# Sub-LayerNorm statistics of a differential-attention layer: sums of squares on four column tiles of the array, and one transpose for all rows

## The chip, the cores and the metric

The kernel runs on one core of one Trainium2 chip. Time is device microseconds (us) of one execution, from the first to the last instruction and what lies around it; the figure before is the median of three runs. The engines are named as the profile names them: PE (TensorE's matmuls), PEld (its weight loads), DVE (VectorE), ACT (ScalarE), POOL (GpSimd) and SP, the engine whose queue issues most of the DMAs.

## What is computed

Two transformer layers over 512 latent tokens and 256 context tokens of width 1024, each followed by a squared-ReLU MLP. Layer 0 uses windowed attention, layer 1 differential attention. The change is in layer 1, in the normalisation of each head's output over its 128 channels:

```python
a = diff_weights(qblk, k_all).astype(v.dtype)          # softmax 1 - lam * softmax 2
ox = einsum('bhqk,bkhe->bqhe', a, v_all)               # 8 heads of 128 channels
...
o32 = o.astype(jnp.float32)
o32 = o32 * lax.rsqrt(jnp.mean(jnp.square(o32), axis=-1, keepdims=True) + SUBLN_EPS)
o32 = o32 * subln_g * (1.0 - lam_init)
return o32.astype(o.dtype).reshape(B, n, H * 2 * d) @ wo
```

All products run in float32 split in a high and a low part, so that most matmuls come in threes (lines 318 to 320).

## The kernel before

The order of PE's instructions is written out by a small scheduler of the kernel's own (`Flow`). Jobs are Python generators that yield the conditions on which they go on; the scheduler keeps a clock that advances by an estimated cost of each PE step (`fl.pe`, with `mm(n)` for one matmul of n columns) and models the other engines' work by estimated costs as well (`dv`, `ac`, `gp`). At each point the job of the highest priority whose conditions hold by that clock emits its next matmuls. So a changed estimate can change the order of everything behind it. The other engines' instructions are put in order by the framework's own scheduling.

In layer 1 four kinds of job share PE for each of the 8 heads (0 to 7). `proj1` projects the head's Q, K and V, six blocks of 128 tokens with 24 matmuls each (`qkv_ps`, 384 columns wide for the four latent blocks and 256 for the two context blocks). `post1` evicts a block: V, then rope on DVE and POOL, then high and low parts of K (`sk`) and Q (`sq`), which PE transposes (`kT_ps`, line 1229, and `qT_ps`, line 1244). `scores1` makes the scores (`s_ps`, line 1324), their minimum on DVE and their exponential on ACT. `att1` transposes the weights (`pT_ps`, line 1389) and multiplies them with V (`o_ps`, line 1361). While head n is in `att1`, `proj1` and `post1` work on head n+1.

The normalisation ends `att1`. The head's output lies transposed: channels on the 128 partitions, 512 tokens along the free dimension (`oraw`). POOL squares it (`osq`). PE sums over the partitions with a matmul against a column of ones: `selT[:, hg, 0:NG]` has ones in column `hg` alone, so the sum of the first head of a pair (`hg` 0) lands in row 0 and that of the second in row 1 of `rms_ps`, over two partitions and 512 columns (line 1418). DVE copies (first head) or adds (second head) the two rows to `rms_sb`. After the second head of a pair, four transposes bring each 128 tokens of `rms_sb` to the partitions (`rmsT`, line 1432), DVE adds epsilon in `rr`, POOL takes the power -1/2, PE transposes back (`rmsB`), and a matmul spreads each row over the partitions (`rms_bc`), by which DVE scales `oraw`. So `rms_ps` runs 8 times and `rmsT` in four groups.

A side job, `resid1`, works on the residual during the projection of heads 1 to 4, one step after each latent block's `kT_ps`: POOL multiplies and adds in `rs_x`, SP stores the piece (`x_res`) and fetches the next. After every fourth step two vectors are loaded (`rs_g`, `rs_b`) and scaled on DVE, and those loads are issued when POOL has read the old ones.

Of the kernel before, what the change touches and what calls it, by code (L numbers as in the profile page):

```python
# [13 lines left out]
F32 = mybir.dt.float32  # L14
F32R = mybir.dt.float32r
AF = mybir.ActivationFunctionType
ALU = mybir.AluOpType
AX = mybir.AxisListType

P = 128  # L20
# [20 lines left out]
NG = 2  # L41
# [167 lines left out]
def dve(n):  # L209
    return n / 960 + 0.067  # L210
# [6 lines left out]
def pool2(n):  # L217
    return n * 0.0022 + 0.12


def mm(n):
    return max(n / 2400 + 0.003, 0.108)
# [12 lines left out]
def hybrid_block(ctx: ExitStack, tc: tile.TileContext, t: dict, out: bass.AP):  # L235
    nc = tc.nc
# [8 lines left out]
    fl = Flow()  # L245
# [6 lines left out]
    def psm(name):  # L252
        return ps.tile([P, 512], F32, name=name, tag="m", bufs=4)

    def f(x):
        return x.bitcast(F32)


    def dv(n, deps, fn, lat=LAT, **kw):
        fn(**kw)  # L260
        return fl.op("D", dve(n), deps, lat)
# [5 lines left out]
    def gp(us, deps, fn, lat=LAT, **kw):  # L267
        fn(**kw)  # L268
        return fl.op("G", us, deps, lat)
# [11 lines left out]
    def load_const(name, shape, pool=None):  # L281
        tl = (pool or const).tile(shape, F32, name="c_" + name, tag="c_" + name)
        nc.sync.dma_start(out=tl, in_=t[name])
        return tl
# [40 lines left out]
    ident = f(identr)  # L325
# [156 lines left out]
    def split(n, dep, src, hi, lo, a_deps=(), lat=LAT):  # L482
        a = ac(n, [dep] + list(a_deps), nc.scalar.copy, out=hi, in_=src)
        return a, dv(n, [a], nc.vector.tensor_tensor, lat=lat, out=lo, in0=src, in1=f(hi), op=ALU.subtract)
# [62 lines left out]
    def hx_tiles(pool, nm, tok=TOK):  # L547
        return [pool.tile([P, 2, 2, tok], F32R, name=nm, tag="A", bufs=4) for _ in range(4)]
# [621 lines left out]
    apool = ctx.enter_context(tc.tile_pool(name="apool1", bufs=4, reuse_waits="tile"))  # L1170
    late = ctx.enter_context(tc.tile_pool(name="late", bufs=1))
    oT = hx_tiles(apool, "oT1", SEQ)
    selT = load_const("selT", [P, 4, 4])
    id4 = const.tile([4, 4], F32R, name="id4")
    nc.scalar.copy(out=id4, in_=ident[0:4, 0:4])
    sublg = load_const("sublnT", [P, 1])
# [1 line left out]
    with tc.tile_pool(name="attn1", bufs=1, reuse_waits="tile") as pool:  # L1178
# [15 lines left out]
        st = {"att": -1, "S": -1, "proj": -1}  # L1194
# [158 lines left out]
        def att1(hd_, R):  # L1353
# [3 lines left out]
            def av(kp, qp, pt_, _, xi):  # L1357
                for pl, vl in ((0, 0), (0, 1), (1, 0)):
                    for a in range(2):
                        kb = kp * 2 + a  # L1360
                        nc.tensor.matmul(out=po[:, qp * 256:(qp + 1) * 256], lhsT=vt[:, kb, vl],
                                         rhs=pt_[:, pl, a * 256:a * 256 + 256],
                                         start=(kp == 0 and pl == 0 and vl == 0 and a == 0),
                                         stop=(kp == 2 and pl == 1 and a == 1))
                p = fl.pe(6 * mm(256))
                xS1.give(xi, p)
                return p
# [4 lines left out]
            while i < 6 or pend:  # L1372
# [4 lines left out]
                if room():  # L1377
# [7 lines left out]
                    for a in range(2):  # L1385
                        for qi in range(2):
# [3 lines left out]
                                                in_=es[qp * 2 + qi][0][:, kb * P:(kb + 1) * P], identity=ident)  # L1390
                    p = fl.pe(4 * mm(P))
# [9 lines left out]
                else:  # L1401
                    p = av(*pend.pop(0))
# [6 lines left out]
            osq = pool.tile([P, 512], F32, name="osq", tag="oraw", bufs=3)  # L1409
            g = gp(pool2(512), [a], nc.gpsimd.tensor_tensor, out=osq, in0=oraw, in1=oraw, op=ALU.mult)  # L1410
            hg = hd_ % NG
            if hg == 0:
                st["rms"] = pool.tile([NG, 512], F32, name="rms_sb", tag="rms_sb", bufs=1)
            rms_sb = st["rms"]
            yield [g, sm_.ok]
            rp = psm("rms_ps")
            slot = sm_.take()
            nc.tensor.matmul(out=rp[0:NG, :], lhsT=selT[:, hg, 0:NG], rhs=osq, start=True, stop=True)
            p = fl.pe(4 * mm(512))
            if hg == 0:  # L1420
                d = dv(512, [p], nc.vector.tensor_copy, out=rms_sb, in_=rp[0:NG, :])
            else:
                d = dv(512, [p], nc.vector.tensor_tensor, out=rms_sb, in0=rms_sb, in1=rp[0:NG, :], op=ALU.add)
            sm_.give(slot, d)
            raws.append(oraw)
            if hg < NG - 1:
# [1 line left out]
            yield [d, sm_.ok]  # L1428
            pr = psm("rmsT")
            slot = sm_.take()  # L1430
            for qb in range(4):
                nc.tensor.transpose(out=pr[:, qb * NG:qb * NG + NG], in_=rms_sb[:, qb * P:(qb + 1) * P],
                                    identity=ident[0:NG, 0:NG])
            p = fl.pe(4 * mm(NG))
            rr = small.tile([P, 4 * NG], F32, name="rr", tag="rr", bufs=1)
            ep = small.tile([P, 4 * NG], F32, name="ep", tag="ep", bufs=1)
            s0 = st["s0"][hd_ // NG].rearrange("p q g -> p (q g)")
            dv(8, [], nc.vector.scalar_tensor_tensor, out=ep, in0=s0, scalar=EPS, in1=s0, op0=ALU.mult, op1=ALU.mult)
            d = dv(8, [p], nc.vector.scalar_tensor_tensor, out=rr, in0=pr[:, 0:4 * NG], scalar=1.0 / P, in1=ep,
                   op0=ALU.mult, op1=ALU.add)  # L1440
            sm_.give(slot, d)
            g = gp(0.3 + 0.17 * 4 * NG, [d], nc.gpsimd.tensor_tensor, out=rr, in0=rr, in1=mhalf[:, 0:4 * NG], op=ALU.pow)
            yield [g, sm_.ok]
# [4 lines left out]
            p = fl.pe(4 * mm(P))  # L1448
            rh = pool.tile([NG, 512], F32R, name="rh", tag="rms_sb", bufs=1)
            rl = pool.tile([NG, 512], F32R, name="rl", tag="oraw", bufs=3)  # L1450
            _, d = split(512, p, pb[0:NG, :], rh, rl)
            sm_.give(slot, d)
            for g in range(NG):
# [4 lines left out]
                                 start=True, stop=False)  # L1458
                nc.tensor.matmul(out=bc, lhsT=id4[0:NG, g:g + 1].broadcast_to([NG, P]), rhs=rl,
                                 start=False, stop=True)  # L1460
                p = fl.pe(2 * mm(512))
# [3 lines left out]
                       op1=ALU.mult)  # L1465
# [92 lines left out]
def _rope_tables():  # L1558
    rows = SEQ // GRID_W
    row = np.repeat(np.arange(rows, dtype=np.float32), GRID_W)  # L1560
    col = np.tile(np.arange(GRID_W, dtype=np.float32), rows)
    nf = HD // 4
    inv = (np.float32(ROPE_BASE) ** (-np.arange(nf, dtype=np.float32) / np.float32(nf))).astype(np.float32)
    ang = np.concatenate([row[:, None] * inv, col[:, None] * inv], axis=-1)
    c, s = np.cos(ang).astype(np.float32), np.sin(ang).astype(np.float32)

    def lay(a):
        return np.ascontiguousarray(a.reshape(NXB, P, HD).transpose(1, 0, 2))

    return lay(np.concatenate([c, c], -1)), lay(np.concatenate([-s, s], -1))  # L1570


def _layout(i):
    a = {k: np.asarray(v) for k, v in i.items()}
    C = np.ascontiguousarray
    r = {}
    xx = np.concatenate([a["x"][0], a["ctx"][0]], axis=0)
    r["xtok"] = C(xx.reshape(NTB, P, D))
    r["xT"] = C(xx.T.reshape(KT, P, TOK).transpose(1, 0, 2))
    r["cT"] = C(np.stack([a["c"][0], a["c_ctx"]], -1).reshape(KT, P, 2).transpose(1, 0, 2))  # L1580
    r["w_adaT"] = C(a["w_ada"].reshape(2, D, 6, KT, P).transpose(0, 2, 3, 4, 1))
    r["w_ada"] = C(a["w_ada"].reshape(2, 2, 4, P, 6, 4, 256).transpose(0, 4, 5, 1, 3, 2, 6).reshape(2, 6, 4, 2, P, 1024))
    r["badaT"] = C(a["b_ada"].reshape(2, 6, KT, P).transpose(3, 0, 1, 2))
    ln = np.stack([a["ln1_g"], a["ln1_b"], a["ln2_g"], a["ln2_b"]], 1)
    r["lnrow"] = C(ln)
    r["lnT"] = C(ln.reshape(2, 4, KT, P).transpose(3, 0, 1, 2))
    r["a_wkv"] = C(np.concatenate([a["a_wk"][0], a["a_wv"][0]], -1).reshape(2, 4, P, 256).transpose(0, 2, 1, 3)
                   .reshape(2, P, 1024))

    def half(w):  # L1590
        return C(w.reshape(4, 2, P, 2, 512).transpose(3, 0, 2, 1, 4).reshape(2, 4, P, 1024))

    r["a_wq"] = half(a["a_wq"][0])
    r["a_wo"] = half(a["a_wo"][0])
    r["b_wo"] = half(a["b_wo"][0])
    bw = np.stack([a[n][0].reshape(4, 2, P, B_HEADS, P) for n in ("b_wq", "b_wk", "b_wv")], 4)
    r["b_w"] = C(bw.transpose(3, 0, 2, 1, 4, 5).reshape(B_HEADS, 4, P, 768))
    r["w1"] = C(a["mlp_w1"].reshape(2, KT, P, 32, P).transpose(0, 3, 2, 1, 4).reshape(2, 32, P, 1024))
    r["w2"] = C(a["mlp_w2"].reshape(2, 4, 4, 2, P, 2, 512).transpose(0, 1, 5, 2, 4, 3, 6).reshape(2, 4, 2, 4, P, 1024))
    r["a_sink"] = C(a["a_sink"])  # L1600
    r["lamv"] = C(np.stack([a["b_lq1"][0], a["b_lk1"][0], a["b_lq2"][0], a["b_lk2"][0]], 0).reshape(1, 4 * HD))
    r["sublnT"] = C(a["b_subln_g"].reshape(P, 1))
    r["cosT"], r["sinT"] = _rope_tables()
    r["ident"] = np.eye(P, dtype=np.float32)
    q, k = np.arange(P)[:, None], np.arange(P)[None, :]
    z = np.zeros((P, P), np.float32)
    tl = np.where(q > k, np.float32(1e30), np.float32(0)).astype(np.float32)
    tr = np.where(k > q, np.float32(1e30), np.float32(0)).astype(np.float32)
    r["mask"] = C(np.stack([tl, z, tr, z, z, z], 1))
    selT = np.zeros((P, 4, 4), np.float32)  # L1610
    for g in range(4):
        selT[:, g, g] = 1
    r["selT"] = selT
    return r
# [12 lines left out]
```

## Time and profile before

| | |
|---|---|
| median of 3 runs | 1721.53 us (1721.34 to 1722.16) |
| profiled execution | 1723.21 us, its span 1721.4 us |
| TensorE clock granted, mean | 0.986 |
| attention of layer 1 | about 960 to 1310 us of the span |
| first `rms_ps` of heads 0 to 7 starts at | 996.8, 1040.9, 1090.0, 1131.9, 1177.6, 1216.5, 1258.9, 1296.7 us |
| DVE busy from 960 to 1310 | 237.6 us |

Rows of the timeline give the start, the length, the engine, the line and the operation with its tiles, and in brackets the idle time of the engine before the row and what ended it. A row of the grouped views gives the count, the busy time, the mean length in ns and the idle time before. A row of a table of stretches gives the stretch, its length, the busy time and the number of instructions of PE, PEld, DVE, ACT and POOL, then the granted clock, the DMA share and the GB/s. Matmuls overlap in the pipeline, so one of them takes less of PE than its own length; the distance between two starts is what counts.

### The profile page before, as it was taken

What the parts mean: (1) busy time and instruction counts of PE and PEld (TensorE: products, weight loads), DVE (VectorE), ACT (ScalarE), POOL (GpSimd) and SP (SyncE); (2) the same over time, 40 slices, a digit from 0 to 9 for tenths busy, and PEclk for the clock granted to TensorE, in tenths of its full rate; (3) what the DMA queues carried; (4) which work ended last, traced back from release to release, by engine and by line L of the source; (5) the groups of instructions that cost most, each with busy time, mean ns of one, the idle gap of its engine ahead of it and who ended that gap; (6) DMA issues with size and microseconds to landing.
All of it is one profiled execution on the core that took longest, in us unless ns stands there. A gap on an engine that the chain in (4) does not pass through costs nothing.

```text
span 1721.4 us, 23369 instructions
## 1 busy us (share of the span) xinstructions
PE 1640.2 (95%) x9093; PEld 1360.0 (79%) x9093; DVE 962.3 (56%) x1811; ACT 657.8 (38%) x1281; POOL 344.9 (20%) x314
## 2 busy tenths in 40 slices
PE   6899999999999999999999999999989799999998
PEld 4787567788788888878878988888977788888886
DVE  3665677677755544444446767676765543233336
ACT  3455455462223212302316555455551533223230
POOL 1343444200001101243220122220100000203422
PEclk9999999999999999999999999999999899999999
DMA  9111451243433434324323122211132214232321
GB/s 361 38 50 32 147 178 44 98 158 119 159 134 110 147 122 135 111 98 147 98 64 111 50 68 62 68 47 37 47 110 98 99 62 135 74 117 79 111 86 49
DMA packets 57240, 174.74 MB, mean 102 GB/s; under 512 B 7145, under 2 KB 13097, under 8 KB 57129
## 3 DMA queue, kind: packets, MB, share of 16 engines
q1 hardware_dynamic: 57128, 173.25, 29.9%
q8 instruction: 71, 1.16, 0.3%
q14 instruction: 41, 0.33, 0.1%
HBM read 165.32 MB, written 7.90 MB: 101 GB/s over the span
## 4 chain that ended last, share of the span: by engine, by line
PE 74%; DVE 10%; issue 5%; ACT 4%; POOL 3%; DMA 3%; SPq 0%; POOLq 0%; DVEq 0%; ACTq 0%
PE y_ps L320 10%; PE y_ps L319 10%; PE y_ps L318 10%; PE h_ps L318 8%; PE h_ps L319 8%; PE h_ps L320 8%; PE o_ps L1014 2%; PE qkv_ps L318 2%; PE qkv_ps L319 2%; PE qkv_ps L320 2%; PE s_ps L1324 2%; DVE e L260 2%; PE pT_ps L1028 2%; DVE w_l L260 2%; PE s_ps L981 1%
## 5 line engine op out<-in xcount | busy, mean ns | idle before, releaser
L264 ACT CAST w_h<-w_raw 128x1024 fp32r<-128x1024 f32 (+1 forms) x185 | 186.8, 1014 | 431.1 <-PE y_ps L320 214.3
L260 DVE TENSOR_TENSOR w_l<-w_raw,w_h 128x1024 fp32r<-128x1024 f32 (+1 forms) x185 | 222.8, 1210 | 226.5 <-ACT w_h L264 225.9
L319 PE MATMUL y_ps<-w_l,hid 128*128 128x512 f32 x640 | 252.9, 395 | 1.9 <-DVE w_l L260 1.9
L320 PE MATMUL y_ps<-w_h,hid 128*128 128x512 f32 x640 | 252.9, 395 | 0.6 <-DVE hid L260 0.5
L318 PE MATMUL y_ps<-w_h,hid 128*128 128x512 f32 x640 | 253.1, 395 | 0.0
L268 POOL TENSOR_TENSOR relu<-relu 128x768 f32<-128x768 f32 (+1 forms) x48 | 81.4, 1695 | 613.9 <-ACT relu L264 613.9
L320 PE MATMUL h_ps<-hx0m,w_l 128*128 128x256 f32 (+1 forms) x528 | 176.9, 335 | 0.8 <-DVE w_l L260 0.8
L318 PE MATMUL h_ps<-hx0m,w_h 128*128 128x256 f32 (+1 forms) x528 | 177.1, 335 | 0.0
L319 PE MATMUL h_ps<-hx0m,w_h 128*128 128x256 f32 (+1 forms) x528 | 176.8, 335 | 0.0
L319 PEld LDWEIGHTS y_ps<-w_l,hid 128*128 128x128 f32 x640 | 120.4, 188 | 31.1 <-DVE w_l L260 3.2
L320 PEld LDWEIGHTS y_ps<-w_h,hid 128*128 128x128 f32 x640 | 120.4, 188 | 30.2 <-DVE hid L260 1.9
L318 PEld LDWEIGHTS y_ps<-w_h,hid 128*128 128x128 f32 x640 | 120.4, 188 | 28.6 <-ACT hid L264 0.2
L318 PE MATMUL qkv_ps<-w_h,hx 128*128 128x384 f32 (+1 forms) x384 | 128.1, 334 | 0.0
L319 PE MATMUL qkv_ps<-w_l,hx 128*128 128x384 f32 (+1 forms) x384 | 123.5, 322 | 1.2 <-DVE w_l L260 1.2
L320 PE MATMUL qkv_ps<-w_h,hx 128*128 128x384 f32 (+1 forms) x384 | 123.4, 321 | 0.0
L268 POOL TENSOR_TENSOR e<-e,sm 128x512 f32<-128x512 f32 (+2 forms) x96 | 95.6, 1011 | 127.4 <-DVE sm L260 104.2
L318 PE MATMUL h_ps<-hx1m,w_h 128*128 128x512 f32 (+1 forms) x288 | 108.2, 376 | 3.6 <-ACT relu L264 3.6
L320 PEld LDWEIGHTS h_ps<-hx0m,w_l 128*128 128x128 f32 x528 | 100.0, 189 | 12.5 <-DVE w_l L260 1.6
L319 PEld LDWEIGHTS h_ps<-hx0m,w_h 128*128 128x128 f32 x528 | 99.9, 189 | 11.3
L318 PEld LDWEIGHTS h_ps<-hx0m,w_h 128*128 128x128 f32 x528 | 99.9, 189 | 11.1
L319 PE MATMUL h_ps<-hx1m,w_h 128*128 128x512 f32 (+1 forms) x288 | 107.7, 374 | 0.0
L320 PE MATMUL h_ps<-hx1m,w_l 128*128 128x512 f32 (+1 forms) x288 | 107.6, 374 | 0.0
(225 smaller groups left out, 3131.2 us busy)
## 6 DMA issues: line engine op xcount, KB each, us to landing
w_raw<-in_w SPq DMA_DIRECT2D x128, 512.0 KB, 3.4
w_raw<-in_w_adaT SPq DMA_DIRECT2D x56, 512.0 KB, 3.3
w_raw<-in_w_ada SPq DMA_DIRECT2D x24, 512.0 KB, 4.3
w_raw<-in_b_w SPq DMA_DIRECT2D x32, 384.0 KB, 3.2
raw<-in_w_ada SPq DMA_DIRECT2D x16, 512.0 KB, 9.5
w_raw<-in_a_wq SPq DMA_DIRECT2D x8, 512.0 KB, 6.9
w_raw<-in_a_wo SPq DMA_DIRECT2D x8, 512.0 KB, 3.7
w_raw<-in_b_wo SPq DMA_DIRECT2D x8, 512.0 KB, 4.4
```

The lines of the kernel that those rows point to most:

```text
L260: fn(**kw)
L264: fn(**kw)
L268: fn(**kw)
L318: nc.tensor.matmul(out=o, lhsT=lh, rhs=rh, start=start, stop=False)
L319: nc.tensor.matmul(out=o, lhsT=lh, rhs=rl, start=False, stop=False)
L320: last["pe"] = nc.tensor.matmul(out=o, lhsT=ll, rhs=rh, start=False, stop=stop)
L981: nc.tensor.matmul(out=sp[:, 512:512 + CTX], lhsT=q_, rhs=kT[:, kvh, hl, SEQ:TOK], start=(hl == 0), stop=(hl == 1))
L1014: nc.tensor.matmul(out=po[odd * HD:odd * HD + HD, 0:256], lhsT=vv[:, kb, kvh], rhs=pt_[:, odd * 256:odd * 256 + 256], start=(i == 0), stop ...
L1028: nc.tensor.transpose(out=pp[:, c * P:(c + 1) * P], in_=es[j][:, i * P:(i + 1) * P], identity=ident)
L1324: nc.tensor.matmul(out=sp[:, c0:c1], lhsT=qTt[:, tt, hl, qb * P:(qb + 1) * P], rhs=kS[:, tt, c0:c1], start=(hl == 0), stop=(hl == 1))
```

## The change

The sums of squares are computed by four matmuls of 128 columns, one for each block of 128 tokens, in place of one of 512. Each has a stationary operand of 32 columns and writes to 32 partitions of its own, so that the four use the four column strips of the array. `selT` has 32 columns for it, of which column `hg` holds ones; the rows 2 to 31 of each strip are zeros. `rms_sb` becomes 128 partitions by 128 columns: row 32 q + g is head g of the pair, token block q. One 128x128 transpose replaces the four, and `rr` picks the columns 32 q + g.

```diff
-    selT = load_const("selT", [P, 4, 4])
+    selT = load_const("selT", [P, NG, 32])
...
-                st["rms"] = pool.tile([NG, 512], F32, name="rms_sb", tag="rms_sb", bufs=1)
+                st["rms"] = pool.tile([P, P], F32, name="rms_sb", tag="rms_sb", bufs=1)
...
-            nc.tensor.matmul(out=rp[0:NG, :], lhsT=selT[:, hg, 0:NG], rhs=osq, start=True, stop=True)
-            p = fl.pe(4 * mm(512))
+            for qb in range(4):
+                nc.tensor.matmul(out=rp[32 * qb:32 * qb + 32, 0:P], lhsT=selT[:, hg], rhs=osq[:, qb * P:(qb + 1) * P],
+                                 start=True, stop=True)
+            p = fl.pe(4 * mm(128))
             if hg == 0:
-                d = dv(512, [p], nc.vector.tensor_copy, out=rms_sb, in_=rp[0:NG, :])
+                d = dv(128, [p], nc.vector.tensor_copy, out=rms_sb, in_=rp[:, 0:P])
             else:
-                d = dv(512, [p], nc.vector.tensor_tensor, out=rms_sb, in0=rms_sb, in1=rp[0:NG, :], op=ALU.add)
+                d = dv(128, [p], nc.vector.tensor_tensor, out=rms_sb, in0=rms_sb, in1=rp[:, 0:P], op=ALU.add)
...
-            for qb in range(4):
-                nc.tensor.transpose(out=pr[:, qb * NG:qb * NG + NG], in_=rms_sb[:, qb * P:(qb + 1) * P],
-                                    identity=ident[0:NG, 0:NG])
-            p = fl.pe(4 * mm(NG))
+            nc.tensor.transpose(out=pr[:, 0:P], in_=rms_sb, identity=ident)
+            p = fl.pe(mm(P))
...
-            d = dv(8, [p], nc.vector.scalar_tensor_tensor, out=rr, in0=pr[:, 0:4 * NG], scalar=1.0 / P, in1=ep,
-                   op0=ALU.mult, op1=ALU.add)
+            d = dv(8, [p], nc.vector.scalar_tensor_tensor, out=rr.rearrange("p (q g) -> p q g", g=NG),
+                   in0=pr[:, 0:P].rearrange("p (q g) -> p q g", g=32)[:, :, 0:NG], scalar=1.0 / P,
+                   in1=ep.rearrange("p (q g) -> p q g", g=NG), op0=ALU.mult, op1=ALU.add)
...
-    selT = np.zeros((P, 4, 4), np.float32)
-    for g in range(4):
+    selT = np.zeros((P, NG, 32), np.float32)
+    for g in range(NG):
```

The estimates of the scheduler's clock change with it: `4 * mm(128)` for `4 * mm(512)`, and one `mm(P)` for `4 * mm(NG)`. Up to head 0's sums the order of all engines is the same; behind them it differs at several places.

The first is on VectorE, in the stretch between the sums of head 0 and the next `kT_ps`. `vt` and `sk` are the low parts of V and K of a context block of head 1, `rs_g` and `rs_b` the residual's vectors:

```order
 L260 TENSOR_TENSOR vt_8449<-qkv_ps,vt_8449 128x128
 L260 TENSOR_SCALAR rs_g<-rs_g 128x256
+L260 COPY rms_sb<-rms_ps 128x128
 L260 TENSOR_SCALAR rs_b<-rs_b 128x256
-L260 COPY rms_sb<-rms_ps 2x512
 L260 TENSOR_TENSOR sk<-qkv_ps,sk 128x2x64
 L260 TENSOR_TENSOR w_l<-w_raw,w_h 128x768 x3
```

The copy of the sums has moved from behind `rs_b` to ahead of it; at head 1 the addition moves in the same way.

The second is on PE behind head 1's `rms_ps`, where the next `kT_ps` stood after six `qkv_ps` matmuls. Before:

```order
L320 MATMUL qkv_ps<-w_h,hx_7757 128x256
L1229 MATMUL kT_ps<-identr,sk 128x128 x2
L318 MATMUL qkv_ps<-w_h,hx_7757 128x256
L319 MATMUL qkv_ps<-w_l,hx_7757 128x256
L320 MATMUL qkv_ps<-w_h,hx_7757 128x256
```

and now, twelve `qkv_ps` matmuls behind `rms_ps`:

```order
L320 MATMUL qkv_ps<-w_h,hx_7757 128x256
L1434 MATMUL rmsT<-identr,rms_sb 128x128
L1229 MATMUL kT_ps<-identr,sk 128x128 x2
L318 MATMUL qkv_ps<-w_h,hx_7757 128x256
L319 MATMUL qkv_ps<-w_l,hx_7757 128x256
```

Six `qkv_ps` have moved ahead of `kT_ps`, and `rmsT`, which stood six matmuls behind it, now stands directly ahead of it. Behind head 0's sums the same six have moved, without `rmsT`.

The third is on PE ahead of head 2's sums, where head 3's blocks are transposed (`kT_ps`, `qT_ps`) between head 2's products (`o_ps`). Before:

```order
L1361 MATMUL o_ps<-pT,vt_8976 128x256 x12
L1229 MATMUL kT_ps<-identr,sk 128x128 x2
L1244 MATMUL qT_ps<-identr,sq 128x128 x4
L1361 MATMUL o_ps<-pT,vt_8976 128x256 x6
L1229 MATMUL kT_ps<-identr,sk 128x128 x2
L1244 MATMUL qT_ps<-identr,sq 128x128 x4
L318 MATMUL qkv_ps<-w_h,hx_7757 128x384
```

and now, from the last of twelve `qkv_ps` matmuls that stand between the first pair of transposes and this one:

```order
L320 MATMUL qkv_ps<-w_h,hx_7757 128x384
L1229 MATMUL kT_ps<-identr,sk 128x128 x2
L1244 MATMUL qT_ps<-identr,sq 128x128 x4
L1389 MATMUL pT_ps<-identr,e_9669 128x128
L1389 MATMUL pT_ps<-identr,e_9747 128x128
```

Two pairs of transposes that stood six `o_ps` apart are now twelve `qkv_ps` apart, and the third pair stands between the last two groups of `o_ps`. Ahead of head 4's sums the same has happened. The order between `rms_bc` and the next `rms_ps` at heads 2 and 4 is now the one that head 6 has in the kernel before; head 6's own rows change to a third order, in which more `qkv_ps` stand between the transposes.

## The prediction

> **What bounds the kernel now.** I read the page first, then busy time by stretch, then the waits of the stretch that the change touches, then its timeline.
>
> ```profile
> span 1721.4 us, 23369 instructions
> PE 1640.2 (95%) x9093; PEld 1360.0 (79%) x9093; DVE 962.3 (56%) x1811; ACT 657.8 (38%) x1281; POOL 344.9 (20%) x314
> PE 74%; DVE 10%; issue 5%; ACT 4%; POOL 3%; DMA 3%; SPq 0%; POOLq 0%; DVEq 0%; ACTq 0%
> 960.00:1310.00 350.00, 331.25 (x2111) 298.87 (x2112) 237.56 (x482) 182.39 (x418) 59.04 (x72) 0.98 0.21 67
> 1310.00:1721.00 411.00, 390.96 (x1760) 318.52 (x1758) 178.60 (x223) 124.68 (x186) 74.44 (x52) 0.98 0.27 89
> PE kT_ps L1229 <- DVE sk L260: 12.0, 15, 3.2
> ```
>
> PE is busy 95% of the span and makes 74% of the chain that ended last. In the attention stretch, 960 to 1310, it is busy 331.25 of 350 us: some 19 us are idle there, and the largest single cause is the transpose of K (`kT_ps`) waiting for VectorE's `sk`: 12.0 us in 15 waits. Behind 1310 the MLP is a dense PE stream, so whatever PE gains in attention moves the end by as much. The sum below therefore follows PE alone.
>
> **The rows that are cut.** The changed operations, and the rows whose shapes are nearest to the new ones:
>
> ```profile
> L1418 PE MATMUL rms_ps<-osq,c_selT 128*2 128x512 f32 x16 | 8.2, 592 | 0.0
> L1432 PE MATMUL rmsT<-identr,rms_sb 2*128 2x2 f32 x16 | 1.8, 213 | 0.0
> L260 DVE COPY rms_sb<-rms_ps 2x512 f32<-2x512 f32 x4 | 2.7, 677 | 0.5 <-PE rms_ps L1418 0.4
> L260 DVE TENSOR_TENSOR vt<-qkv_ps,vt 128x128 fp32r<-128x128 f32 x43 | 12.3, 286 | 19.2 <-ACT vt L264 19.2
> ```
>
> One `rms_ps` matmul leaves two records, so 16 records are 8 heads. What it takes from PE is not its duration but the distance between its neighbours:
>
> ```profile
> 1296.40 0.40 PE L320 MATMUL y_ps<-w_h,oT 128*128 128x512 f32 x1
> 1296.73 1.02 PE L1418 MATMUL rms_ps<-osq,c_selT 128*2 128x512 f32 x2
> 1297.68 0.50 PE L318 MATMUL y_ps<-w_h,oT 128*128 128x512 f32 x1
> 1298.02 0.39 PE L319 MATMUL y_ps<-w_l,oT 128*128 128x512 f32 x1
> ...
> 1298.94 0.40 PE L320 MATMUL y_ps<-w_h,oT 128*128 128x512 f32 x1
> 1299.27 0.41 PE L1432 MATMUL rmsT<-identr,rms_sb 2*128 2x2 f32 x4
> 1299.61 0.50 PE L318 MATMUL y_ps<-w_h,oT 128*128 128x512 f32 x1
> 1299.94 0.39 PE L319 MATMUL y_ps<-w_l,oT 128*128 128x512 f32 x1
> ```
>
> Four steps of `y_ps` lie between 1298.02 and 1298.94, so one is 0.23. From 1296.40 to 1298.02 are 1.62 us; less two steps, `rms_ps` takes **1.16**. From 1298.94 to 1299.94, less two steps, the four `rmsT` take **0.54**.
>
> The new form, four matmuls on four column strips of 32, stands in this trace already: the first layer's `ada_ps` puts eight of 256 columns there.
>
> ```profile
> L360 PE MATMUL ada_ps<-raw,cs x128: 379/403/636, 6.1 to 51.4; 128*32 128x256 f32 x128
> 27.41 0.28 PE L320 MATMUL kv_ps<-w_h,hx 128*128 128x256 f32 x1
> 27.52 0.38 PE L384 MATMUL ada_t<-identr,ada_rows 128*128 128x128 f32 x2
> 27.84 1.07 PE L360 MATMUL ada_ps<-raw,cs 128*32 128x256 f32 x16
> 28.84 0.50 PE L318 MATMUL q_ps<-w_h,hx 128*128 128x512 f32 x1
> 29.17 0.39 PE L319 MATMUL q_ps<-w_l,hx 128*128 128x512 f32 x1
> ```
>
> From 27.41 to 29.17 are 1.76 us. Less 0.11 for the `kv_ps` step, 0.23 for the `q_ps` step and about 0.23 for two transposes, 16 records take some 1.19 us, though each lasts 0.38 or more: the strips do run at once. The new `rms_ps` has 8 records of half the columns. I take half, **0.59**, because per record is the dearer of the two readings (columns alone would give a quarter, 0.30); the other end is the whole 1.19. It saves 0.57 a head (bounds -0.03 and 0.86), 8 x 0.57 = 4.6. For `rmsT`, four in 0.41 with the last 0.20 long are 0.07 apart; three fewer save 0.21, and 128 columns in place of 2 give back a few hundredths: I take 0.18 (0 to 0.42), 4 x 0.18 = 0.7. Heads 0 and 1 get nothing of this, since both run straight into a wait whose end VectorE sets: less 2 x 0.57 and 0.18, 1.3. The rows cut are worth 5.3 - 1.3 = **4.0 us**.
>
> On VectorE an eviction goes from 677 ns to about the 286 of a 128x128 one, 8 x 0.39 = 3.1 us of busy time. Except at heads 0 and 1 PE's matmuls hide that, so it counts nothing. The larger `selT` load stands among the first layer's loads, long ahead of its use in the second; the two SP rows that swap (`x_res` and `rs_x`) have a third buffer behind them: nothing for both.
>
> **The waits at heads 0 and 1.** PE, and VectorE at head 0:
>
> ```profile
> 1002.00 0.47 PE L1229 MATMUL kT_ps<-identr,sk 128*128 128x128 f32 x2 [3.24 <-DVE sk L260]
> 1045.38 0.33 PE L1229 MATMUL kT_ps<-identr,sk 128*128 128x128 f32 x2 [2.57 <-DVE sk L260]
> 999.20 0.29 DVE L260 TENSOR_SCALAR rs_g<-rs_g 128x256 f32<-128x256 f32 x1 [1.65 <-DMA rs_g<-in_lnrow]
> 1000.78 0.29 DVE L260 TENSOR_SCALAR rs_b<-rs_b 128x256 f32<-128x256 f32 x1 [1.29 <-DMA rs_b<-in_lnrow]
> 1000.99 0.67 DVE L260 COPY rms_sb<-rms_ps 2x512 f32<-2x512 f32 x1
> 1001.59 0.27 DVE L260 TENSOR_TENSOR sk<-qkv_ps,sk 128x128 fp32r<-128x128 f32 x1
> ```
>
> VectorE stands at `rs_b` for a DMA; behind it queue the copy, then `sk`, and PE waits for `sk`. In the new order the copy stands ahead of `rs_b`, inside its 1.29 us of idle time, so `sk` can start at 1000.99: 0.60 earlier. Six `qkv_ps` matmuls (0.11 each, 0.66) also move from behind `kT_ps` to before it, into the wait. That is 1.26 at each head; at head 1 `rmsT` too moves into the wait, and its 0.54 vanishes: **3.1 us**. What is late next is `rs_b`'s DMA, which the change does not touch.
>
> **The order of heads 2 and 4.** The scheduler's clock runs by estimated costs, so a shorter `rms_ps` reshuffles what follows. Ahead of heads 2 and 4's sums, pairs of `kT_ps` and `qT_ps` that stood close together are now spaced by 12 `qkv_ps`, row for row as head 6 has them before the change. So before's head 6 shows what the new order costs:
>
> ```profile
> 1226.00:1259.00 33.00, 32.84 (x223) 30.79 (x223) 25.10 (x54) 19.05 (x45) 3.98 (x5) 1.00 0.09 29
> 1054.00:1090.00 36.00, 33.23 (x220) 31.05 (x219) 25.25 (x55) 18.28 (x44) 8.59 (x11) 1.00 0.11 34
> 1142.00:1178.00 36.00, 34.14 (x219) 32.19 (x218) 24.47 (x55) 18.69 (x46) 3.94 (x5) 0.95 0.03 11
> 1076.55 0.37 PE L1229 MATMUL kT_ps<-identr,sk 128*128 128x128 f32 x2 [0.65 <-DVE sk L260]
> 1078.34 0.45 PE L1244 MATMUL qT_ps<-identr,sq 128*128 128x128 f32 x3 [1.34 <-DVE sq L260]
> 1163.09 0.36 PE L1229 MATMUL kT_ps<-identr,sk 128*128 128x128 f32 x2 [0.61 <-DVE sk L260]
> 1164.36 0.45 PE L1244 MATMUL qT_ps<-identr,sq 128*128 128x128 f32 x3 [0.81 <-DVE sq L260]
> 1002.00:1005.00 3.00, 3.00 (x15) 3.00 (x16) 0.94 (x2) 1.20 (x2) 0.00 (x0) 0.50 0.52 167
> 1165.00:1168.00 3.00, 3.00 (x16) 2.91 (x15) 0.30 (x1) 1.09 (x3) 0.00 (x0) 0.59 0.00 0
> ```
>
> In the first three rows PE idles 0.16 us at head 6, 2.77 at head 2, 1.86 at head 4. Head 4's granted clock is also 0.95 over 36 us, because the 3 us behind its waits ran at 0.59 (as the 3 us behind head 0's wait ran at 0.50): about 1.7 us more. Head 4 is worth 1.86 + 1.65 - 0.16 = 3.35. Head 2 has 8.59 us of POOL work against head 6's 3.98 (the residual's pieces), which may hold up the rope that feeds `sk`; of its 2.6 I take half, 1.3 (0 to 2.6). Together **4.7 us**.
>
> [...]
>
> The other nine or so waits of `kT_ps` (12.0 less the priced 3.24, 2.57, 0.65, 0.61) I leave at their sum. Some go; new ones come: at head 2 `rs_g` and `rs_b` now stand ahead of `vt`, `rms_sb` and `sk` on VectorE (0 to the 3.24 of head 0), and `rmsB` follows `rmsT` after 12 `qkv_ps` in place of 18 at heads 1 and 3.
>
> **Sum.** 4.0 + 3.1 + 4.7 = 11.8 us. The profiled execution took 1723.2 (its span 1721.4), which becomes 1711.4; the median of the runs, 1721.5, is 1.7 lower and becomes **1709.7**.
>
> **Rivals.**
> *The slow-clock stretches of heads 0 and 1 go as well*: their waits shrink from 3.24 and 2.57 to about 2.5 and 1.4. For it: 0.31 + 0.65 + 1.34 at head 2 brought no slow stretch. Against: 1.43 at head 4 did. Worth 2 x 1.65: 1706.4.
> *Entering and leaving the strips costs, not the columns*: the four take `ada_ps`'s whole 1.19, and the six counted heads lose 0.57 each: 1713.1. For it: nothing in the trace separates the two parts of 1.19. [...]
> *The new order only moves the waits*: the two last terms are nothing, leaving 4.0: 1717.5. For it: 56% of VectorE is used, and it serves everyone in order. Against: head 6.
> *All is absorbed*: VectorE's chains set every head: 1721.5.
> *Slower: the strips run one after another* at the record's 0.403, so the change doesn't do what it says. Eight are 3.22 us, 2.06 more than now at six heads (the waits of heads 0 and 1 swallow theirs), 12.4, against 3.1 + 4.7 + 0.5 gained: 1725.6. It decides from 2.5 us for the four. Against: 16 records in 1.07 us at 27.84.
>
> **How the numbers follow.** A measurement of this kernel tells about 0.2%, 3.4 us, from no change. Chances: forecast 0.40, clock 0.17, strips' fixed price 0.10, moved waits 0.18, absorbed 0.10, slower 0.05. The moved waits sit on the boundary, so 0.08 of theirs counts as same: faster 0.77, same 0.18, slower 0.05. The range runs from 1703 (the clock rival with head 2 in full and the cheap strips) to 1719 (just past the moved waits), and leaves out the last two.
>
> **What would show it.** Eight `rms_ps` groups of 8 records within 0.5 to 0.6 us; one `rmsT` record a pair of heads; `rms_sb` evictions near 290 ns; at heads 0 and 1 a wait for `sk` that starts later and ends 0.6 earlier; heads 2 and 4 with under 1.5 us of PE idle and no clock below 1.00. The forecast is wrong if head 2 or 4 shows a wait over 2 us, if head 6, whose rows also change, loses its 0.16, or if slow stretches appear where there were none.

## The result and the profile after

The changed kernel takes **1712.31 us** (median of 6 runs, 1708.07 to 1715.99), the kernel before 1721.43 beside it (6 runs, 1718.65 to 1723.99): a ratio of 0.9946, 95% interval 0.9934 to 0.9957, or 9.1 us less. The forecast was 1709.7, or 11.8 less. The execution that was profiled took 1715.99, the slowest of the six; the profiled one of before took 1723.21.

The page after, span, engines and the shares of the chain that ended last:

```profile
span 1714.2 us, 23438 instructions
PE 1634.3 (95%) x9129; PEld 1359.1 (79%) x9129; DVE 957.7 (56%) x1811; ACT 658.1 (38%) x1281; POOL 345.9 (20%) x314
PE 75%; DVE 9%; issue 5%; ACT 4%; POOL 3%; DMA 3%; SPq 0%; POOLq 0%; DVEq 0%; ACTq 0%
```

PE is the bound as before. Its busy time is 5.9 us less, the span 7.2 us less. Next the groups of the changed operations, then head 7's sums and transposes among the dense `y_ps` matmuls on the timeline:

```profile
L1420 PE MATMUL rms_ps<-osq,c_selT 128*32 128x128 f32 x64 | 3.4, 285 | 0.0
L260 DVE COPY rms_sb<-rms_ps 128x128 f32<-128x128 f32 x4 | 1.1, 284 | 1.2 <-PE rms_ps L1420 1.2
L1434 PE MATMUL rmsT<-identr,rms_sb 128*128 128x128 f32 x4 | 1.1, 278 | 0.9 <-ACT w_h L264 0.9
```

```profile
1289.40 0.40 PE L320 MATMUL y_ps<-w_h,oT 128*128 128x512 f32 x1
1289.72 0.43 PE L1420 MATMUL rms_ps<-osq,c_selT 128*32 128x128 f32 x8
1290.08 0.51 PE L318 MATMUL y_ps<-w_h,oT 128*128 128x512 f32 x1
1290.42 0.39 PE L319 MATMUL y_ps<-w_l,oT 128*128 128x512 f32 x1
...
1291.35 0.40 PE L320 MATMUL y_ps<-w_h,oT 128*128 128x512 f32 x1
1291.58 0.27 PE L1434 MATMUL rmsT<-identr,rms_sb 128*128 128x128 f32 x1
1291.61 0.48 PE L318 MATMUL y_ps<-w_h,oT 128*128 128x512 f32 x1
1291.92 0.39 PE L319 MATMUL y_ps<-w_l,oT 128*128 128x512 f32 x1
```

Read as before: from 1290.42 to 1291.35 are four `y_ps` steps, 0.93 us, so two are 0.465. From 1289.40 to 1290.42 are 1.02; less two steps, `rms_ps` takes 0.55 (1.16 before). From 1291.35 to 1291.92, less two steps, `rmsT` takes 0.10 (0.54 before).

Where the time went is read from the starts of `rms_ps` of heads 0 to 7, which after the change are 997.27, 1039.89, 1083.65, 1124.09, 1165.95, 1204.15, 1251.46 and 1289.72. The forecast's terms fall on the same intervals:

| from head to head | before, us | after, us | change | forecast |
|---|---|---|---|---|
| 0 to 1 | 44.04 | 42.62 | -1.42 | -1.26 (head 0's wait) |
| 1 to 2 | 49.12 | 43.76 | -5.36 | -3.1 (head 1's wait 1.26, `rmsT` 0.54, order at head 2 1.3) |
| 2 to 3 | 41.85 | 40.44 | -1.41 | -0.57 |
| 3 to 4 | 45.76 | 41.86 | -3.90 | -4.1 (0.75 for the rows, order at head 4 3.35) |
| 4 to 5 | 38.90 | 38.20 | -0.70 | -0.57 |
| 5 to 6 | 42.41 | 47.31 | **+4.90** | -0.75 |
| 6 to 7 | 37.80 | 38.26 | +0.46 | -0.57 |
| 0 to 7 | 299.88 | 292.45 | -7.43 | -10.92 |

Up to head 5 the change gained more than forecast, 12.79 against 9.6; then it gave back 5.36 where 1.32 more was expected. By kind, from head 0's sums to head 7's, first before and then after the change (the second number of a row is PE's busy time):

```profile
996.85:1296.73 299.88, 281.58 (x1809) 255.33 (x1809) 204.42 (x417) 156.86 (x360) 47.70 (x59) 0.98 0.20 63
997.27:1289.72 292.45, 276.26 (x1842) 255.18 (x1841) 201.89 (x417) 157.23 (x360) 48.82 (x59) 0.98 0.20 64
```

PE is busy 5.3 us less and idles 2.1 us less (16.2 for 18.3), and the time at half clock is the same, four times 3.41 us, partly in other places. Put the same way, the forecast's 10.92 are 4.5 of busy time (seven `rms_ps` and three groups of `rmsT`), 4.7 of idle time and 1.7 of the clock. What stands behind head 5, on PE and VectorE, now:

```profile
1208.55 0.60 PE L1449 MATMUL rmsB<-identr,rr 128*2 128x128 f32 x4
1211.47 0.37 PE L1229 MATMUL kT_ps<-identr,sk 128*128 128x128 f32 x2 [2.32 <-DVE sk L260]
1207.21 2.70 DVE L260 TENSOR_TENSOR w_l<-w_raw,w_h 128x768 fp32r<-128x768 f32 x3 [0.47 <-ACT w_h L264]
1209.86 0.68 DVE L260 TENSOR_TENSOR rl<-rmsB,rh 2x512 fp32r<-2x512 f32 x1
1210.47 0.27 DVE L260 TENSOR_TENSOR vt<-qkv_ps,vt 128x128 fp32r<-128x128 f32 x1
1211.12 0.29 DVE L260 TENSOR_TENSOR sk<-qkv_ps,sk 128x128 fp32r<-128x128 f32 x1 [0.39 <-ACT sk L264]
```

and before:

```profile
1221.83 0.60 PE L1447 MATMUL rmsB<-identr,rr 128*2 128x128 f32 x4
1224.38 0.33 PE L1229 MATMUL kT_ps<-identr,sk 128*128 128x128 f32 x2
1223.96 0.27 DVE L260 TENSOR_TENSOR sk<-qkv_ps,sk 128x128 fp32r<-128x128 f32 x1
```

VectorE needs about as long in both: `sk` starts 2.57 us behind `rmsB` now and 2.13 before. But before, twelve `qkv_ps` matmuls stood between `rmsB` and `kT_ps` and covered it; now `kT_ps` stands directly behind `rmsB`, and PE waits 2.32 us. What follows is dearer than the wait itself, by the table of stretches (granted clock third from the end):

```profile
1213.00:1217.00 4.00, 4.00 (x12) 2.86 (x13) 2.61 (x5) 1.26 (x3) 0.00 (x0) 0.58 0.63 212
1217.00:1221.00 4.00, 4.00 (x16) 3.96 (x15) 2.00 (x3) 1.95 (x4) 0.00 (x0) 0.57 0.01 2
1130.00:1166.00 36.00, 35.83 (x244) 33.59 (x245) 26.94 (x57) 20.49 (x49) 3.97 (x5) 1.00 0.11 33
1048.00:1084.00 36.00, 35.50 (x244) 33.12 (x243) 27.03 (x58) 20.55 (x48) 10.02 (x13) 1.00 0.18 59
```

The 8 us behind the wait ran at 0.58 and 0.57, which loses 4 x 0.42 + 4 x 0.43 = 3.4 us of PE's full speed. The last two rows are the 36 us ahead of head 4's and head 2's sums, as they were read before: PE idles 0.17 and 0.50 us there (1.86 and 2.77 before), at a clock of 1.00. The waits of PE in the attention stretch, by line and cause:

```profile
PE kT_ps L1229 <- DVE sk L260: 8.5, 6, 2.3
PE rmsB L1449 <- POOL rr L268: 1.6, 2, 1.0
```

`kT_ps` waits 8.5 us in 6 places, down from 12.0 in 15: many small waits went, and fewer, longer ones are left. Around head 6 two of 1.44 and 1.42 us stand where before had 0.15 and 1.22. `rmsB`'s two waits for POOL's power are new.

### The profile page after: what moved, and what is told of

Same layout as the page of the kernel before. It is cut to its first block, busy times and chain, and to the rows that moved or that the text cites. A ratio compares the mean times of both kernels' runs of the same rounds, so it can differ in the third digit from the quotient of the medians.

```text
span 1714.2 us, 23438 instructions
## 1 busy us (share of the span) xinstructions
PE 1634.3 (95%) x9129; PEld 1359.1 (79%) x9129; DVE 957.7 (56%) x1811; ACT 658.1 (38%) x1281; POOL 345.9 (20%) x314
## 4 chain that ended last, share of the span: by engine, by line
PE 75%; DVE 9%; issue 5%; ACT 4%; POOL 3%; DMA 3%; SPq 0%; POOLq 0%; DVEq 0%; ACTq 0%
PE y_ps L320 10%; PE y_ps L319 10%; PE y_ps L318 10%; PE h_ps L318 8%; PE h_ps L319 8%; PE h_ps L320 8%; PE o_ps L1014 2%; PE qkv_ps L318 2%; PE s_ps L1324 2%; PE qkv_ps L319 2%; PE qkv_ps L320 2%; DVE e L260 2%; DVE w_l L260 2%; PE pT_ps L1028 2%; ACT w_h L264 1%
```

## The experiments

The theory after the result: the terms of the forecast hold, and a new term is the order behind head 5. The rivals: the gain is the rows alone and the order worth nothing; the order is as good as forecast and something else took 2.7 us back. Each ratio stands to the kernel before on the same chip; "0 to 7" is the distance from head 0's `rms_ps` to head 7's (299.88 before, 292.45 after the change).

### Rows without the new order

The changed kernel with the old estimates, so that PE's rows stand in the old order:

```diff
-            p = fl.pe(4 * mm(128))
+            p = fl.pe(4 * mm(512))
...
-                d = dv(128, [p], nc.vector.tensor_copy, out=rms_sb, in_=rp[:, 0:P])
+                d = dv(512, [p], nc.vector.tensor_copy, out=rms_sb, in_=rp[:, 0:P])
...
-            p = fl.pe(mm(P))
+            p = fl.pe(4 * mm(NG))
```

> The new matmuls, transpose and evictions, but the scheduler's estimates as before, so that PE's order is that of the kernel before row for row (VectorE's copy of the sums still moves ahead of rs_b at heads 0 and 1). Theory (the sum of the prediction, with the sizes that the changed kernel's trace shows): rms_ps takes 0.55 in place of 1.16 and rmsT 0.10 in place of 0.54; heads 0 and 1 absorb theirs, so 6 x 0.61 + 3 x 0.44 = 5.0, and the waits there end 0.6 earlier, 1.2: together 6.2 us, 1715.2 against 1721.4. Rival (the order makes the gain, the rows cut are absorbed by VectorE's chains): within 1.5 us of the kernel before.

Measured: 1714.2 us, ratio 0.9958 (0.9945 to 0.9972), 6.7 less than the 1720.87 of before; 0 to 7 in 295.42. The theory's size held (6.2 expected). The waits at heads 0 and 1 stayed at 2.90 and 2.58 (3.24 and 2.57 before), so shorter rows alone do not remove them. The profiled execution understates the gain: it has 20.5 us at half clock from head 0 to head 7 where the one of before has 13.7, which is 3.4 us of full speed.

### The new order without the rows

The kernel before with the new estimates (the same three edits the other way): PE's order is that of the change, row for row, and `rms_ps` and `rmsT` are the old ones. VectorE's copy at head 0 stays behind `rs_b`.

> The old matmul, transposes and evictions with the new estimates, so that PE's order is that of the changed kernel row for row. Theory: what is left of the 9.1 us, some 3 us: 1718.5. Its PE idle is under 1 us at heads 2 and 4 and over 2 us at head 5, as in the changed kernel. Rival (the order makes the gain): 1713.

Measured: 1715.21 us, ratio 0.9970 (0.9961 to 0.9980), 5.7 less; 0 to 7 in 295.84. That lies between the two. The order is worth something by itself, and it brought head 5's wait with it (2.38 us, and 5.1 us lost to the clock behind it). The two parts sum to more than the whole (6.7 + 5.7 against 9.1); one overlap is on record: from head 0 to head 1 each alone saves most of what both save (0.98 and 1.21 against 1.42). Where the rest goes stays open.

### The old order from head 5 on

The changed kernel with new estimates for heads 0 to 4 only:

```diff
-            p = fl.pe(4 * mm(128))
+            p = fl.pe(4 * mm(128 if hd_ < 5 else 512))
...
-                d = dv(128, [p], nc.vector.tensor_copy, out=rms_sb, in_=rp[:, 0:P])
+                d = dv(128 if hd_ < 5 else 512, [p], nc.vector.tensor_copy, out=rms_sb, in_=rp[:, 0:P])
...
-            p = fl.pe(mm(P))
+            p = fl.pe(mm(P) if hd_ < 5 else 4 * mm(NG))
```

> The changed kernel with the old estimates at heads 5 to 7 alone, so that PE's order is the changed one up to head 4 and that of the kernel before behind it. Theory (the changed kernel gives back at heads 5 and 6 what the order won at heads 2 and 4): the 2.32 us wait of kT_ps at head 5 goes with one or two slow-clock stretches of 1.7 each behind it, and about 1.5 us of waits at head 6: 4 to 7 us faster than the changed kernel, 1705 to 1708. Rival (the waits only move on): within 1.5 us of the changed kernel, 1712.

Measured: 1703.47 us, ratio 0.9908 (0.9892 to 0.9923); 0 to 7 in 285.29, 7.16 less than the change, of which 5.80 lie between heads 5 and 6 (41.51) and 1.31 between 6 and 7 (36.95). The waits of this kernel and the stretch behind head 5's sums:

```profile
PE kT_ps L1229 <- DVE sk L260: 4.6, 5, 1.9
1199.00:1211.00 12.00, 12.00 (x87) 10.57 (x86) 7.65 (x14) 6.48 (x14) 2.01 (x2) 1.00 0.45 144
```

No idle time and a clock of 1.00 for 12 us: the wait of 2.32 and the stretch behind it are gone, and with them 7 to 9 us of the whole (this set of runs and a second one below, against 1712.31). This settles where the miss comes from: the order from head 5 on.

### One load of the residual's vectors

`rs_g` and `rs_b` are loaded and scaled once instead of four times, so the residual uses the first quarter's vectors in all four:

```diff
-                if tb == 0:
+                if n == 0:
```

> The changed kernel, but the residual's vectors rs_g and rs_b are loaded and scaled once in place of four times, so all four quarters use the first quarter's (this leaves out part of the computation). PE's order is the same. Theory (rs_b's DMA sets the waits of kT_ps at heads 0 and 1): the 2.3 us wait at head 0 goes down to under 1 with the slow-clock stretch of 1.7 behind it, and about 0.8 of 1.7 at head 1: 3 to 5 us faster, 1707.5 to 1709.5. Rival (VectorE's chain of vt and sk sets them): under 1 us faster.

Measured: 1705.02 us, ratio 0.9909 (0.9895 to 0.9922), 7.3 less than the change, more than the 3 to 5 expected; 0 to 7 in 287.01. VectorE and PE at head 0, first after the change, then without the loads:

```profile
1001.61 0.33 PE L1229 MATMUL kT_ps<-identr,sk 128*128 128x128 f32 x2 [2.31 <-DVE sk L260]
999.56 0.29 DVE L260 TENSOR_SCALAR rs_g<-rs_g 128x256 f32<-128x256 f32 x1 [1.60 <-DMA rs_g<-in_lnrow]
999.77 0.28 DVE L260 COPY rms_sb<-rms_ps 128x128 f32<-128x128 f32 x1
1000.97 0.29 DVE L260 TENSOR_SCALAR rs_b<-rs_b 128x256 f32<-128x256 f32 x1 [0.92 <-DMA rs_b<-in_lnrow]
1001.18 0.28 DVE L260 TENSOR_TENSOR sk<-qkv_ps,sk 128x128 fp32r<-128x128 f32 x1
```

```profile
997.20 0.29 PE L1229 MATMUL kT_ps<-identr,sk 128*128 128x128 f32 x2
995.93 0.28 DVE L260 COPY rms_sb<-rms_ps 128x128 f32<-128x128 f32 x1
996.35 0.29 DVE L260 TENSOR_TENSOR sk<-qkv_ps,sk 128x128 fp32r<-128x128 f32 x1
```

The change moved the copy into the wait for `rs_b` and left that wait standing; `sk` still queues behind it. Without the DMA PE does not wait. What the change left at heads 0 and 1 was this load, and it was worth more than the waits alone, since head 0's half-clock stretch went too.

### An earlier `rmsT`

The kernel with the old order from head 5 on, with the measured 0.55 us as the estimate of `rms_ps` for heads 0 to 4; `rmsT` at heads 1 and 3 moves six matmuls forward:

```diff
-            p = fl.pe(4 * mm(128 if hd_ < 5 else 512))
+            p = fl.pe(0.55 if hd_ < 5 else 4 * mm(512))
```

> The kernel with the old order from head 5 on, and the estimate of rms_ps set to the 0.55 us that it was measured to take, for heads 0 to 4. Only one thing moves against that kernel: rmsT of heads 1 and 3 stands six qkv_ps matmuls (about 0.7 us) earlier, so that rr is ready earlier and rmsB should no longer wait for POOL's power (0.54 at head 1, 1.03 at head 3 before). Theory, that these two waits are paid in full because PE is the bound: 1.0 to 1.5 us less than the kernel with the old order from head 5 on (1703.5), so about 1702. Rival, that the waits only move into the next kT_ps, whose sk is late anyway: 1703.5, within 0.5.

Measured: 1703.68 us, ratio 0.9899 (0.9884 to 0.9915): no gain, so the theory missed. 0 to 7 took 285.07, 0.22 less. Both waits of `rmsB` are gone, as meant. But head 1's wait is now one piece:

```profile
1040.61 0.30 PE L1434 MATMUL rmsT<-identr,rms_sb 128*128 128x128 f32 x1 [1.70 <-DVE rms_sb L260]
1041.00:1045.00 4.00, 4.00 (x25) 3.91 (x23) 2.83 (x6) 2.15 (x4) 2.30 (x1) 0.57 0.43 131
```

The kernel it is compared with waited 1.07 + 0.44 + 0.53 there, at full clock. Now 1.70 us in one go has 4 us at 0.57 behind it, 1.7 lost: 0.34 and 1.04 of waits were saved and 1.7 paid.

### Four matmuls on one strip

The new order, but the four matmuls of 128 columns all on the same columns of the array, in the old layout of the statistics:

```diff
-            nc.tensor.matmul(out=rp[0:NG, :], lhsT=selT[:, hg, 0:NG], rhs=osq, start=True, stop=True)
+            for qb in range(4):
+                nc.tensor.matmul(out=rp[0:NG, qb * P:(qb + 1) * P], lhsT=selT[:, hg, 0:NG],
+                                 rhs=osq[:, qb * P:(qb + 1) * P], start=True, stop=True)
```

> The order of PE's rows as in the change, but the four matmuls of 128 columns all stand on the same columns of the array (two columns of selT, two partitions of output) and the statistics keep their old layout. Read at head 7 between the dense y_ps matmuls. Theory, that the 0.55 us of the changed kernel come from four strips working at once: the four take one after another what the one of 512 columns took, 1.16 us (at least 1.0). Rival, that shorter matmuls are cheaper by themselves: 0.55 to 0.8. The time should be that of the kernel with the order alone, 1715, and little under it by the rival.

Head 7's sums on the timeline:

```profile
1293.02 0.40 PE L320 MATMUL y_ps<-w_h,oT 128*128 128x512 f32 x1
1293.34 1.03 PE L1419 MATMUL rms_ps<-osq,c_selT 128*2 128x128 f32 x8
1294.31 0.50 PE L318 MATMUL y_ps<-w_h,oT 128*128 128x512 f32 x1
1294.64 0.39 PE L319 MATMUL y_ps<-w_l,oT 128*128 128x512 f32 x1
```

From 1293.02 to 1294.64 are 1.62; less two steps, 1.16 us: the single matmul's. The theory held; the 0.55 is the work of four strips at once, not of shorter matmuls. The one run took 1718.57, within the 1712.88 to 1719.65 of the order alone.

### Head 5's wait filled

The changed kernel with eight matmuls behind head 5's `rmsB` whose results nothing reads:

```diff
+            for k in range(8 if hd_ == 5 else 0):
+                nc.tensor.matmul(out=pb[32:64, 0:P], lhsT=selT[:, 0], rhs=ident, start=True, stop=True)
```

> The changed kernel with eight matmuls added behind head 5's rmsB, where PE waits 2.32 us for kT_ps: float32, 128 columns, into 32 partitions that nothing reads; eight times a quarter of 1.16 are 2.3 us, so they fill the wait and kT_ps should start where it did. Theory, that the half-clock stretch behind this wait (8 us, 3.4 us lost) comes from PE's idle time: the stretch goes, and the time falls by about 3.4 us to 1709 although PE has more to do. Rival, that the clock falls there for another cause than idle time: the stretch stays, and the time is that of the changed kernel, 1712, or up to 2.3 more if the eight push kT_ps back.

Measured: 1710.66 us, ratio 0.9942 (0.9928 to 0.9956); 0 to 7 in 289.10, 3.35 less than the change.

```profile
1208.74 1.93 PE L1452 MATMUL rmsB<-identr,c_selT 128*32 128x128 f32 x16
1212.32 0.37 PE L1229 MATMUL kT_ps<-identr,sk 128*128 128x128 f32 x2 [1.65 <-DVE sk L260]
1213.00:1217.00 4.00, 4.00 (x21) 3.11 (x20) 2.66 (x5) 1.48 (x4) 0.00 (x0) 1.00 0.45 166
1217.00:1221.00 4.00, 4.00 (x25) 3.91 (x24) 3.46 (x7) 2.49 (x5) 0.00 (x0) 1.00 0.02 4
```

In this execution the stretch at half clock is gone, though PE has more to do, as the theory had it. The test doesn't show the cause: `kT_ps` starts 8.50 us behind head 5's sums in place of 7.32, 1.65 us of the wait stayed, and the interval of the ratio overlaps that of the change, so the time of the whole decides nothing. Of the 3.35 us only 1.84 lie between heads 5 and 6; 1.19 lie between heads 6 and 7, where nothing was filled and where this execution has no half-clock stretch behind a wait of 1.93 us while the one of the change has.

### Scaling `rs_g` and `rs_b` later

The kernel with the old order from head 5 on; VectorE scales the two vectors one step of the residual later, and nothing is left out:

```diff
-                        dv(128, [], nc.vector.tensor_scalar, out=gb[k], in0=gb[k], scalar1=ALPHA, scalar2=None,
-                           op0=ALU.mult)
+                        dv(128, [], lambda: None)
...
                 x, q, dst, (g, b) = nxt
+                if n % NXB == 0:
+                    for v in (g, b):
+                        behind(nc.vector.tensor_scalar, after)(out=v, in0=v, scalar1=ALPHA, scalar2=None, op0=ALU.mult)
```

> The kernel with the old order from head 5 on (1703.5), and VectorE scales rs_g and rs_b one step of the residual later, right before POOL needs them, when their DMAs have long landed; everything is still computed and PE's order is unchanged, row for row. Theory, that the waits of heads 0 and 1 are set by rs_b's DMA, behind which sums and sk queue on VectorE: the waits of 1.93 (head 0) and 1.07 + 0.44 (head 1) go, head 0's half-clock stretch with them (1.7), while rmsB's wait at head 1 grows from 0.53 to about 1.0 as where one load was left: 1.93 + 1.51 + 1.7 - 0.5 = 4.6 less, about 1699 (1697 to 1701). Rival, that sk is late there for other reasons, or that POOL and VectorE, whose order also moves elsewhere, lose as much: 1702 to 1705.

Measured: 1702.99 us, ratio 0.9901 (0.9884 to 0.9917): 0.5 less than its base, where 4.6 was expected: the size missed. The waits of `kT_ps` and `rmsT` at heads 0 and 1 and head 0's stretch went; `rmsB`'s grew to 1.03; 0 to 7 took 282.25, 3.0 less. From head 0 to head 1 it gained 1.95 us (40.28 for 42.23), where the wait and the stretch came to 3.6; what took the rest stays open. The profiled execution of the base had come to head 0 at 993.09, this one at 996.33, and with medians from different chips 0.5 us decided nothing. Two more kernels went on one chip, one the base again:

> The kernel with the old order from head 5 on once more, on the same chip as the last one, since its first profiled execution came to head 0 some 3 us earlier than most others. Theory, that this offset is scatter of an execution and not of the kernel: head 0's sums at 995 to 997 us in most executions, head 0 to head 7 again in 285.3 us within 1, the median 1703 to 1706. Rival, that the kernel itself is earlier there: head 0's sums at 993 again.

Measured: 1705.26 us, ratio 0.9902 (0.9885 to 0.9918); head 0's sums at 996.14, 0 to 7 in 286.15. The early start was scatter of one execution.

> Old order from head 5 on, the scaling of rs_g and rs_b one step later, and the estimate 0.55 for rms_ps of heads 0 to 4: PE's order is that of the kernel with the earlier rmsT, VectorE's that of the kernel with the later scaling but for the rmsT rows. Nothing is left out. Theory, that rmsB's two waits of 1.03 at heads 1 and 3 are all that the later scaling left at heads 0 to 3: they go, and no half-clock stretch stands behind heads 0 and 1: head 0 to head 7 in 280.2 us (282.25 less 2.06), and 4 to 5 us less time than the kernel with the old order from head 5 on, run beside it. Rival, that the time saved in attention is taken back elsewhere (the MLP, the start of the layer), as the kernel with the later scaling was 3.0 us shorter from head 0 to head 7 and only 0.5 us in its median: within 1.5 us of the kernel beside it.

Measured: **1699.06 us**, ratio 0.9873 (0.9859 to 0.9888), 6.2 less than the base beside it; 0 to 7 in 280.16 (expected 280.2). The attention stretch (clock third from the end) and the waits of `kT_ps`:

```profile
960.00:1310.00 350.00, 337.39 (x2223) 307.19 (x2222) 246.26 (x504) 183.80 (x418) 60.66 (x73) 1.00 0.22 72
PE kT_ps L1229 <- DVE sk L260: 2.1, 3, 1.1
```

That 280.16 meets the 280.2 is partly luck. Of the 2.09 us less than with the later scaling alone, 0.93 lie between heads 3 and 4, where `rmsB`'s wait went as forecast. Between heads 1 and 2 only 0.05 was gained: `rmsB`'s wait went there too, but a new one of 0.74 stands at `s_ps`. And 1.15 lie between heads 6 and 7, which the edit doesn't touch: no half-clock stretch came behind the wait of 1.93 us in this execution. So both moves together gave 6.2 us against the base in medians on one chip, with no run of one among the other's; what the earlier `rmsT` adds by itself is shown at head 3 alone, where it also paid in the kernel without the later scaling (40.74 for 41.86). With 1699.06 this kernel beats both the one before (1721.62 beside it) and the change.

## Why the prediction was right, and where it was off

- **The rows that are cut**, 4.0. `rms_ps` was put at 0.59 by the reading that each record has its price; it takes 0.55, and the kernel with one strip shows that the strips are what saves it. The rival of a fixed price for the strips (1.19) and the slower one (eight records in line, 3.22) are out. `rmsT` was put at 0.18 saved, 0.42 at most; it saves 0.44, since one transpose takes 0.10 in the stream where 0.36 was left for it. The copy on VectorE takes 284 ns (286 forecast).
- **The waits at heads 0 and 1**, 3.1. Head 0: 1.42 for 1.26. Of the 0.83 us that `sk` starts earlier behind the sums, 0.60 is the copy, as forecast, and 0.23 an earlier end of the wait for `rs_b` (3.70 us behind the sums for 3.93), which the change does not explain. "What is late next is `rs_b`'s DMA" is shown by the kernel with one load. At head 1 the waits fell from 2.57 to 0.93 + 0.78, which is less than forecast, and `rmsB` added 0.54; but its half-clock stretch went (1.7), which the forecast had as a rival. Head 0's stayed.
- **The order of heads 2 and 4**, 4.7. Head 4's interval gave 3.90 of the 4.1 with its rows; its slow stretch went. Head 2 kept 0.50 of its 2.77 us of idle, so 2.27 where half (1.3) was taken.
- **The failing step**: "The other nine or so waits of `kT_ps` [...] I leave at their sum. Some go; new ones come". (By the count of the view there were eleven: 15 less 4.) The new ones were not looked for behind head 4. At head 5 the new order puts `kT_ps` directly behind `rmsB`, and the rows of before held the price: VectorE's `sk` 2.13 us behind `rmsB`, under cover of twelve `qkv_ps`. The term was put at 0; it cost 4.9 us from head 5 to 6 where 0.75 of gain was expected, and head 6 lost its 0.16. Two of the signs that the prediction named against itself came with it: head 6's loss, and a slow stretch where there was none. Taking it back gave 0 to 7 in 285.29, 7.16 less than the change.

So the forecast had the rows and the waits at heads 0 to 4 about right, but that the sum came out near it is partly luck: two errors met, 3.2 us more gained up to head 5 than forecast (head 1's clock, head 2's idle time), and 6.7 less behind it (5.65 from head 5 to 6, 1.0 from 6 to 7; the two go together, since ten matmul records moved from ahead of head 6's sums to behind them). Of the 4.7 us of idle time in the forecast 2.1 came in the profiled execution, of the 1.7 of clock nothing, of the 4.5 of busy time 5.3: most of the gain is busy time.

## What to carry to other kernels

A kernel whose order comes from estimated costs reacts to a changed estimate everywhere behind it: go through each place where the new order takes matmuls out from between a producer on another engine and its consumer, and price each as "what covered this wait before", not only the places where the order improves. A wait of PE cost twice here: the 2.32 us at head 5 themselves, and 3.4 us lost to the clock of 0.58 and 0.57 behind them. So compare traces with the half-clock stretches counted, since one of 3.41 us more or less was 1.7 us here, which the edit may have nothing to do with. And look for an engine that stands for a DMA with other work queued behind it: after the change VectorE stood 0.92 us for `rs_b`'s DMA at head 0, `sk` came behind it, and PE waited 2.31 us for `sk`; placing the operation that needs the DMA a step later took 3.0 us out of the attention.

## What the runs showed of the hardware

From 940 to 1690 us the profiled execution before the change has six stretches of 3.41 us and one of 6.83 at a granted clock of 0.50, the one after it three of each; the kernel with the order alone has 10.24 us behind head 5's wait. They lose 1.7, 3.4 and 5.1 us of full speed. Those priced above stood behind waits of PE (3.24 us at head 0 before, 2.32 at head 5 after), but the length of the wait does not settle it. The same waits at head 2 (0.31, 0.65 and 1.34 us) had a clock of 1.00 behind them before the change (first row) and one of 0.66 over 5 us (1075 to 1080) in the kernel with the rows alone:

```profile
1075.00:1082.00 7.00, 4.69 (x31) 4.24 (x31) 3.68 (x8) 4.03 (x10) 3.00 (x4) 1.00 0.19 59
1075.00:1080.00 5.00, 4.20 (x20) 4.11 (x21) 0.76 (x2) 1.24 (x3) 1.25 (x2) 0.66 0.18 56
```

The same shows at the wait of 1.93 us of `pT_ps` for `e`. In the kernel with the old order from head 5 on (first two rows) the 4 us from 1261 ran at 0.57; in the fastest kernel (last two) the 4 us from 1259 ran at 1.00:

```profile
1259.94 0.98 PE L1389 MATMUL pT_ps<-identr,e 128*128 128x128 f32 x7 [1.93 <-DVE e L260]
1261.00:1265.00 4.00, 4.00 (x19) 3.71 (x18) 3.72 (x6) 1.47 (x4) 0.00 (x0) 0.57 0.17 43
1258.88 0.98 PE L1391 MATMUL pT_ps<-identr,e 128*128 128x128 f32 x7 [1.93 <-DVE e L260]
1259.00:1263.00 4.00, 4.00 (x31) 3.75 (x31) 3.92 (x7) 2.02 (x4) 0.00 (x0) 1.00 0.17 49
```

Which waits get such a stretch behind them is left open here.
